# Two w_up products kept in PSUM for the convolution, and one difference of norm2 moved behind the broadcast

## The chip, the core and the metric

The kernel runs on one core of a Trainium2 chip. The core has five engines that are used here: TensorE (PE, matrix products into PSUM), VectorE (DVE), ScalarE (ACT), GpSimd (POOL, which works on SBUF) and SyncE (SP, which issues the DMAs). Each engine works through its own queue in order and waits on semaphores for the others. The metric is the device time of one execution in microseconds, as the median over runs; lower is better.

## The reference, cut to what matters

The program is one layer of an encoder with 1024 positions, 1024 channels and a hidden width of 2816: two kinds of attention and a gated merge, then a feed-forward part with a depthwise convolution. Only the second half is touched:

```python
x = x + gate1 * (merged @ w_out)
h2 = rmsnorm(x, g_ffn) * (1 + scale2) + shift2
u = depthwise_conv3(h2 @ w_up) + conv_b          # 1024 -> 5632 channels, 3 taps along the positions
u_val, u_gate = split(u, 2)
x = x + gate2 * ((gelu(u_gate) * u_val) @ w_down)
return rmsnorm(x, g_final)
```

## The kernel before

**Layout.** Channels lie on the 128 partitions, positions along the free dimension in two halves of 512. An fp32 product is made of three fp32r products of a high and a low part (weights high x data high, high x low, low x high). A split into the two parts is a copy on ACT (`L55`, `L768`, `L873`, `L942`) and a subtraction on POOL (`L56`) or DVE (`L769`, `L874`, `L943`).

**w_up, 22 jobs.** A job `t` makes 128 value channels and 128 gate channels over all 1024 positions. It uses a Strassen-like scheme with 7 products (`products`, `STEPS`) in place of 8: each product is 4 x 3 matmuls of 128x128 by 128x512 (`L822` to `L824`). The four results lie in four PSUM banks, called a, b, c, d in `"abcdacd"[j]`, of a pool of six (`pj`, bufs=6). [...] The running sums `t` and `v` are tiles of `wc` in SBUF (5 of them). After product 0, ACT copies bank a into `t` (`L828`). After product 1, DVE adds bank b to `t` (`L830`), after 2 it adds bank c and `t` into `v` (`L832`), after 3 it adds bank d and `v` (`L835`): the second half of the gate channels. After 4, bank a holds the first half of the value channels; after 5, bank c plus `t` is the second half of them (`L840`); after 6, bank d plus `t` is the first half of the gate channels (`L844`). Where the results of `L835` and `L844` go is what `in_psum` says: without it (all w_up jobs) into the `wc` tile of `v` and of `t`; with it (the w_down jobs) back into a PSUM bank, b and d.

**The convolution.** `done` hands each of the four results to `finish`. `conv_in` (`L1012`, ACT) multiplies a half by the middle tap and adds the bias, into a tile `ys` of `big`. `conv_taps` adds the two outer taps in six DVE instructions (`L1018`), each with a half or a part of it as one input and `ys` as the other and the output. The positions are stored so that a neighbour lies 256 columns away or in the other half; the six instructions read 512, 256 or 255 columns. Then gelu on ACT (`L1044`), the product with the value half on DVE (`L1045`), and a store to DRAM (`L1046`) for w_down. The first two jobs (`t < 2`) wait until both halves are there before `conv_in`. In the last job the convolution has a lower priority.

**The weights.** `a_operands` makes the four combinations of a job's weights: sums on POOL (`L786` to `L788`) and DVE (`L795`), and splits on ACT and POOL, in two pairs of buffers.

**norm2, ahead of w_up.** `out_tile` (w_out) leaves for each of 8 channel tiles the scaled second half of the positions in `m2[k]`; the first half is already normalised in `m1[k]`. POOL takes differences `m2[k] = m2[k+4] - m2[k]` for k = 0 to 2 (`L997`), DVE the fourth (`L1003`). PE sums the squares; `rstd_of` makes the reciprocal root (`L94` DVE, `L95` ACT, `L96` DVE); PE broadcasts it over the partitions (`L102`). Then a loop with a fixed order for ACT, DVE and POOL multiplies each `m2[k]` by the broadcast (`L1084`), builds the operands T2 (`L1086`, `L942`, `L943`), T1 (`L1088`, `L768`, `L769`) and T3, and on POOL the start of T4 (`L1095`). PE meanwhile does the two products of jobs 0 and 1 that need only the first half (B11 and B21), in an order that is written out by hand up to the end of this stage.

**What sets the order elsewhere.** Within `manual_schedule` the order is that of the code. Elsewhere a planner lays out each engine's queue when the program is built, by its own durations and by the priority of the code's order; a tile or bank is given out when the planner's simulation finds one free, and the waits for it are put into the program.

**The way into w_down.** Jobs of w_down come straight behind. Their data operands come from the stored activations: `b_operands` takes differences on POOL into `wc` tiles (`L892`) and back (`L893`), and `moved` makes each operand through a copy in a PSUM bank (`L872`), a high part (`L873`) and a low part (`L874`, DVE).

Of the kernel before, what the change touches and what calls it, by code (L numbers as in the profile page):

```python
# [12 lines left out]
OP = mybir.AluOpType  # L13
# [15 lines left out]
def hybrid_encoder(tc, xT, c, w_ada, small, w_in, w_v, p1_bias, p23_bias, na_bias, ln2_mult, ident, w_br, w_out,  # L29
                   w_up, w_down, out):  # L30
    nc = tc.nc
    act, dve, pool, pe, sp = nc.scalar, nc.vector, nc.gpsimd, nc.tensor, nc.sync
# [53 lines left out]
    def add_sums(pcol, sq, first, last, n=4):  # L86

        for t in range(n):
            pe.matmul(pcol[:, t:t + 1], sq[:, t * 128:(t + 1) * 128], ones, start=first and t == 0,
                      stop=last and t == n - 1, skip_group_check=True)  # L90
# [169 lines left out]
    with tc.manual_schedule(engines={e.engine for e in (sp, act, dve, pool, pe)}):  # L260
# [50 lines left out]
        for n in range(24):  # L311
            g, k = divmod(n, 8)
# [542 lines left out]
    def wide(dtype=FT):  # L855
        return keep.tile([128, 512], dtype, name="wc", bufs=5)

    def big(shape, dtype=FT):
        return keep.tile(shape, dtype, name="big", bufs=9)
# [85 lines left out]
    def out_tile(hf, m, sqa, scaled):  # L945

        cols = halves[hf]
        w = out_w.pop()
        if hf + m < KT:
            out_w.append(weights(w_out[(m + 1) % KT], (pool, pool)[hf or m == KT - 1]))  # L950
        p = ps.tile([128, 512], FT, name="pj", bufs=6)
        product(p, w, lambda k: [t[:, k, cols] for t in ms])
        xx = x2[hf][m]
        dve.scalar_tensor_tensor(xx, p, ada[:, 16 + m:17 + m], xx, OP.mult, OP.add)
        sp.dma_start(x_scr[m][:, cols], xx)
        sq = sqa if m == 0 else wide()
        if m == KT - 1:
            dve.tensor_tensor(sq, xx, xx, OP.mult)
        else:
            act.activation(sq, xx, AF.Square)  # L960
        act.activation(scaled, xx, AF.Copy, scale=am2[:, m:m + 1])
        if 0 < m < KT - 1:
            (dve if hf and m > 2 else pool).tensor_tensor(sqa, sqa, sq, OP.add)
        return sq

    def up_load(t):
        raw = []
        for i in range(2):
            r = big([128, KT, 128]) if t in (0,) or t > 1 and t % 2 else wpool.tile([128, KT, 128], FT, name="wraw")
            sp.dma_start(r, w_up[t + FF * i])  # L970
            raw.append(r.rearrange("p (a b) m -> p a b m", a=2))
        return raw
# [16 lines left out]
    m2 = []  # L989
# [10 lines left out]
    late_mm.enter_context(tc.manual_schedule(engines={pe.engine}))  # L1000
    m2.append(half_tile())
    sq = out_tile(1, KT - 1, sqa, m2[KT - 1])
    dve.tensor_tensor(m2[3], m2[7], m2[3], OP.subtract)  # L1003
    mpool.release()
    oppool2 = tc.alloc_tile_pool(name="ops2", bufs=1, side="right", reuse_waits="tile")
    for n in ("T2", "T1", "T3"):
# [3 lines left out]
    with tc.tile_pool(name="up", bufs=2, reuse_waits="tile") as work:  # L1010
        def conv_in(y, t, hf, src):
            act.activation(y[:, halves[hf]], src, AF.Identity, bias=conv[:, 3, t:t + 1], scale=conv[:, 1, t:t + 1])  # L1012

        def conv_taps(y, t, ph):
            w0, w2 = conv[:, 0, t:t + 1], conv[:, 2, t:t + 1]

            def tap(dst, src, wt):
                dve.scalar_tensor_tensor(y[:, dst], src, wt, y[:, dst], OP.mult, OP.add)  # L1018
            tap(slice(256, 768), ph[0], w0)
            tap(slice(768, 1024), ph[1][:, 0:256], w0)  # L1020
            tap(slice(1, 256), ph[1][:, 256:511], w0)
            tap(slice(0, 256), ph[0][:, 256:512], w2)
            tap(slice(256, 768), ph[1], w2)
            tap(slice(768, 1023), ph[0][:, 1:256], w2)

        def up_products(t, st, seq=range(7)):
            u, ys = [{}, {}], {i: big([128, S]) for i in range(2) if t == FF - 1}

            def done(i, hf, src):
                u[i][hf] = src  # L1030
                if len(u[i]) == 1 and t < 2:
                    return
                with tc.high_priority(offset=-300 if t == FF - 1 else 0):
                    finish(i, hf)

            def finish(i, hf):
                if i not in ys:
                    ys[i] = big([128, S])
                for n in range(2) if t < 2 else (hf,):
                    conv_in(ys[i], t + FF * i, n, u[i][n])  # L1040
                if len(u[i]) == 2:
                    conv_taps(ys[i], t + FF * i, u[i])
                if len(u[0]) + len(u[1]) == 4:
                    act.activation(ys[1], ys[1], AF.Gelu_apprx_tanh)  # L1044
                    dve.tensor_tensor(ys[0], ys[0], ys[1], OP.mult)  # L1045
                    sp.dma_start(a_scr[t], ys[0])  # L1046
            return products(st, 4, lambda n, k: late[n][k] if n in late else (ops[n][0][:, k], ops[n][1][:, k]), done,
                            seq)

        raw[1] = up_load(1)  # L1050
        prep = [a_operands(raw.pop(t), 4, lambda t: work, sts[t], dve) for t in range(2)]
        next(prep[0])
        next(prep[1])
        for _ in range(3):
            next(prep[0])
        next(prep[1])
        gens = [up_products(t, sts[t], (0, 4, 1, 2, 3, 5, 6)) for t in range(2)]

        def advance(g):
            for j in g:  # L1060
                if j >= 0:
                    return j

        pcol = ps.tile([128, 512], FT, name="pcol")
        add_sums(pcol, sqa, True, False)
        next(gens[0])
        add_sums(pcol, sq, False, True)
        advance(gens[0])
        bc = bcast(rstd_of(pcol, 4), ps, "pbc")
        advance(gens[1])  # L1070
        advance(gens[0])
        advance(gens[1])

        t2 = big([128, 2, 512])
        t2 = [t2[:, 0], t2[:, 1], wide(), wide()]

        def t_split(n, k, src, b):
            shifted(src, b, ops[n][0][:, k], ops[n][1][:, k])

        with tc.manual_schedule(engines={act.engine, dve.engine, pool.engine}):  # L1080

            for k in range(10):
                if k < 8:
                    dve.tensor_tensor(m2[k], m2[k], bc, OP.mult)  # L1084
                if 1 <= k < 5:
                    dve.tensor_tensor(t2[k - 1], m2[k - 1], m1[k - 1], OP.add)  # L1086
                elif k >= 5 and k < 9:
                    dve.tensor_tensor(m1[k - 5], m2[k - 1], t2[k - 5], OP.subtract)  # L1088
                if 2 <= k < 6:
                    t_split("T2", k - 2, t2[k - 2], shift2[:, 2 + k:3 + k])  # L1090
                elif k >= 6:
                    operand(m1[k - 6], ops["T1"][0][:, k - 6], ops["T1"][1][:, k - 6], dve)
            for k in range(4):
                t_split("T3", k, m2[k], dshift[:, k:k + 1])
                pool.tensor_tensor(m1[4 + k], m1[4 + k], t2[k], OP.subtract)  # L1095
            for k in range(4):
                late["B22"].append((half_tile(FR), half_tile(FR)))
                shifted(m2[4 + k], shift2[:, 4 + k:5 + k], *late["B22"][k])
            for k in range(4):
                late["T4"].append((half_tile(FR), half_tile(FR)))  # L1100
                operand(m1[4 + k], *late["T4"][k], pool)
        for g in gens:
            advance(g)
        late_mm.close()
        for t in range(FF):
            nxt = iter(())
            if t + 2 < FF:
                raw[t + 2] = up_load(t + 2)
            if 0 < t < FF - 1:
                nxt = a_operands(raw.pop(t + 1), 4, lambda t: work, sts[t + 1], last=t + 2 == FF)  # L1110
                next(nxt)
            elif t == 0:
                nxt = prep[1]
            for j in gens[t] if t < 2 else up_products(t, sts[t]):
                if j in (((2, 5), (2, 3, 5))[t] if t < 2 else (1, 2, 5)):
                    next(nxt, None)
                if t == FF - 1 and j == 0:
                    more = b_operands(0, movs[0])
                    next(more)
                if t == FF - 1 and j == 2:  # L1120
                    next(more)
                if t == FF - 1 and j == 3:
                    oppool2.release()
                    work2 = tc.alloc_tile_pool(name="down2", bufs=1, side="right", reuse_waits="tile")
                    reserve(work2, [(n + e, 2048, G) for n in ("B11", "T2", "T1") for e in "hl"]
                            + [("T3h", 2048, G), ("T3l", 2048, G)])
                    for _ in range(3):
                        next(more)
# [204 lines left out]
```

## Time and profile before

| | |
|---|---|
| time, median of three runs | 1574.42 us (1573.51 to 1581.34) |
| profiled execution: time, span | 1572.37 us, 1570.5 us |
| granted TensorE clock, mean | 0.982 |
| PE, DVE, ACT, POOL busy | 1505.5, 1035.6, 779.1, 740.6 us |
| w_up, from 1000 to 1320 us in the span | PE 320.00 of 320.00 us busy |
| conv taps `L1018` with a source in `wc` | 132 of them, mean 933 ns |
| conv taps `L1018` with a source in `pj` | 132 of them, mean 565 ns |

The span runs from the first to the last instruction of the profiled execution; its own time has a little around it. All positions in microseconds are counted from the start of the span. A row of the timeline has the start, the duration (of all instructions merged into the row), the engine, the line, the operation, the tile written and the tiles read, the shapes, the count, and in brackets the idle time before it with the engine and tile that ended the wait. PE's matmuls overlap: their durations of 0.39 us are longer than their spacing. `x` is the name of the tiles of the second half of norm2 too, `big` and `wc` are shared SBUF tiles, `pj` the PSUM banks of the products.

### The profile page before, as it was taken

How to read it: one execution, taken by the hardware profiler on the slowest of the kernel's cores; microseconds unless marked ns; L12 is line 12 of the kernel's file. 1: busy time of each engine (PE TensorE's matmuls, PEld its weight loads, DVE VectorE, ACT ScalarE, POOL GpSimd, SP SyncE). 2: the span in 40 equal slices, each digit the busy share in tenths (PEclk: the TensorE clock that was granted, in tenths of full speed). 3: DMA queues.
4: the chain of work that ended last, by engine and by line, in shares of the span. 5: the costliest groups of instructions: out<-in, count | busy, mean ns of one | idle time of the engine just before them, and what ended most of it. 6: DMA issues, size and time to landing. Idle time of an engine off the chain costs nothing.

```text
span 1570.5 us, 21187 instructions
## 1 busy us (share of the span) xinstructions
PE 1505.5 (96%) x7582; PEld 1267.3 (81%) x7582; DVE 1035.6 (66%) x1873; ACT 779.1 (50%) x1419; POOL 740.6 (47%) x475
## 2 busy tenths in 40 slices
PE   7998899999999999999999888999999999999998
PEld 6787788888888998887778777888888887778777
DVE  7694366576766655535534898776666667877765
ACT  3420466566765766643344454444444446575542
POOL 2310523233324444311145858676666665778621
PEclk8899999999999999999999999999999999999999
DMA  9577632323245565555544212322222224523313
GB/s 374 193 272 282 171 80 93 100 73 107 75 108 144 149 160 139 170 174 172 175 136 141 94 54 81 108 81 81 82 87 87 81 74 144 189 97 122 115 53 108
DMA packets 110001, 205.21 MB, mean 131 GB/s; under 512 B 40356, under 2 KB 55588, under 8 KB 109860
## 3 DMA queue, kind: packets, MB, share of 16 engines
q1 hardware_dynamic: 109624, 203.59, 40.3%
q8 instruction: 60, 0.98, 0.3%
q14 instruction: 45, 0.37, 0.1%
q10 hardware_dynamic: 272, 0.26, 0.1%
HBM read 158.73 MB, written 42.47 MB: 128 GB/s over the span
## 4 chain that ended last, share of the span: by engine, by line
PE 64%; DVE 12%; DMA 8%; POOL 6%; issue 4%; ACT 4%; SPq 1%; DVEq 0%; ACTq 0%; POOLq 0%
PE pj L822 8%; PE pj L823 8%; PE pj L824 8%; PE pj L79 8%; PE pj L77 8%; PE pj L78 8%; DMA g<-gs 2%; DMA wraw<-w_down 2%; PE pj L378 2%; DVE mt L151 2%; DVE big L1018 2%; PE O L672 2%; POOL wsl L56 2%; POOL wlo L56 1%; PE T L660 1%
## 5 line engine op out<-in xcount | busy, mean ns | idle before, releaser
L56 POOL TENSOR_TENSOR wlo<-wraw,whi 128x1024 fp32r<-128x1024 f32 (+1 forms) x77 | 178.9, 2323 | 249.6 <-ACT whi L55 224.4
L79 PE MATMUL pj<-h,wlo 128*128 128x512 f32 x448 | 178.6, 399 | 1.4 <-POOL wlo L56 1.4
L77 PE MATMUL pj<-h,whi 128*128 128x512 f32 x448 | 178.4, 398 | 0.1
L78 PE MATMUL pj<-h,whi 128*128 128x512 f32 x448 | 178.2, 398 | 0.0
L56 POOL TENSOR_TENSOR wsl<-big,wsh 128x1024 fp32r<-128x1024 f32 (+1 forms) x45 | 109.5, 2434 | 48.1 <-ACT wsh L55 48.0
L1018 DVE SCALAR_TENSOR_TENSOR big<-wc,sm,big 128x256 f32<-128x256 f32 (+1 forms) x132 | 116.8, 933 | 17.3 <-ACT big L1012 17.2
L55 ACT ACTIVATE whi<-wraw 128x1024 fp32r<-128x1024 f32 (+1 forms) x79 | 80.7, 1022 | 73.7 <-PE pj L78 30.0
L79 PEld LDWEIGHTS pj<-h,wlo 128*128 128x128 f32 x448 | 84.4, 188 | 16.3 <-POOL wlo L56 1.8
L78 PEld LDWEIGHTS pj<-h,whi 128*128 128x128 f32 x448 | 84.3, 188 | 14.4
L77 PEld LDWEIGHTS pj<-h,whi 128*128 128x128 f32 x448 | 84.4, 188 | 14.2 <-PE pj L79 0.5
L449 POOL TENSOR_TENSOR vv<-vv 96x256 fp32r<-96x256 f32 (+2 forms) x32 | 41.2, 1297 | 102.6 <-ACT vv L448 93.1
L498 ACT ACTIVATE P<-P,st 128x256 f32<-128x256 f32 x128 | 64.3, 503 | 49.6 <-DVE st L497 49.3
L385 POOL TENSOR_SCALAR qb<-qs 128x256 fp32r<-128x256 f32 x32 | 26.4, 851 | 124.0 <-PE S L544 57.9
L497 DVE CUSTOM_DVE_ANT_0 P<-S,bias 128x256 f32<-128x256 f32 x128 | 52.4, 421 | 42.3 <-PE S L544 23.2
L1018 DVE SCALAR_TENSOR_TENSOR big<-pj,sm,big 128x512 f32<-128x512 f32 x132 | 67.9, 565 | 16.1 <-ACT big L1012 16.1
L1012 ACT ACTIVATE big<-wc,sm 128x512 f32<-128x512 f32 x44 | 35.8, 816 | 75.7 <-DVE wc L835 45.3
L56 POOL TENSOR_TENSOR wsl<-wraw,wsh 128x768 fp32r<-128x768 f32 (+1 forms) x23 | 49.9, 2171 | 45.5 <-ACT wsh L55 45.5
L650 POOL TENSOR_SCALAR P<-P,stb 128x288 f32<-128x288 f32 (+1 forms) x32 | 39.9, 1248 | 66.0 <-DVE stb L647 58.8
L55 ACT ACTIVATE wsh<-big 128x1024 fp32r<-128x1024 f32 (+1 forms) x45 | 44.8, 1000 | 37.1 <-POOL big L787 23.6
L1044 ACT ACTIVATE big<-big 128x1024 f32<-128x1024 f32 x22 | 23.3, 1060 | 80.2 <-DVE big L1018 80.2
L503 DVE TENSOR_TENSOR tl<-T,th 128x512 fp32r<-128x512 f32 x64 | 43.7, 688 | 23.9 <-ACT th L502 23.5
L840 DVE TENSOR_TENSOR pj<-pj,wc 128x512 f32<-128x512 f32 x34 | 23.7, 696 | 47.0 <-PE pj L824 46.9
(366 smaller groups left out, 4862.3 us busy)
## 6 DMA issues: line engine op xcount, KB each, us to landing
wraw<-w_in SPq DMA_DIRECT2D x32, 512.0 KB, 4.2
t<-w_ada SPq DMA_DIRECT2D x24, 512.0 KB, 8.0
big<-w_up SPq DMA_DIRECT2D x22, 512.0 KB, 5.9
wraw<-w_up SPq DMA_DIRECT2D x22, 512.0 KB, 3.5
as<-big SPq DMA_DIRECT2D x22, 512.0 KB, 2.6
big<-as SPq DMA_DIRECT2D x22, 512.0 KB, 6.2
wraw<-w_down SPq DMA_DIRECT2D x24, 384.0 KB, 3.7
x<-w_ada SPq DMA_DIRECT2D x16, 512.0 KB, 9.9
```

Of the source, the lines that this page charges most:

```text
L55: act.activation(hi, raw, AF.Copy)
L56: lo_eng.tensor_tensor(lo, raw, f(hi), OP.subtract)
L77: pe.matmul(psum, whi[:, k0 + k], mhi, start=k == 0, stop=False)
L78: pe.matmul(psum, whi[:, k0 + k], mlo, start=False, stop=False)
L79: pe.matmul(psum, wlo[:, k0 + k], mhi, start=False, stop=k == n - 1)
L497: dve.tensor_tensor_reduce(pp, d, bias, -1.0, BIG, OP.add, OP.min, mi)
L498: act.activation(pp, pp, AF.Exp, bias=mi, scale=-1.0, accum_out=li)
L503: dve.tensor_tensor(tl, pt, f(th), OP.subtract)
L822: pe.matmul(psum, whi[:, k], bhi, start=j < 4 and k == 0, stop=False, skip_group_check=True)
L823: pe.matmul(psum, whi[:, k], blo, start=False, stop=False, skip_group_check=True)
L824: pe.matmul(psum, wlo[:, k], bhi, start=False, stop=k == n - 1, skip_group_check=True)
L1018: dve.scalar_tensor_tensor(y[:, dst], src, wt, y[:, dst], OP.mult, OP.add)
```

## The change

From the third job on (`t > 1`), `products` gets `in_psum`: `L835` writes its sum into bank b and `L844` into bank d, and `conv_in` and `conv_taps` read all four halves from PSUM. The first two jobs stay as they were. The other part moves the fourth difference of norm2, `m2[3] = m2[7] - m2[3]` on DVE, from ahead of the reciprocal root into the loop, just before `m2[3]` is multiplied by the broadcast.

```diff
@@ norm2
     sq = out_tile(1, KT - 1, sqa, m2[KT - 1])
-    dve.tensor_tensor(m2[3], m2[7], m2[3], OP.subtract)
     mpool.release()
@@ up_products
             return products(st, 4, lambda n, k: late[n][k] if n in late else (ops[n][0][:, k], ops[n][1][:, k]), done,
-                            seq)
+                            seq, t > 1)
@@ the loop behind the broadcast
             for k in range(10):
+                if k == 3:
+                    dve.tensor_tensor(m2[3], m2[7], m2[3], OP.subtract)
                 if k < 8:
                     dve.tensor_tensor(m2[k], m2[k], bc, OP.mult)
```

## The prediction, made before the changed kernel was run

> **What bounds the kernel now.** I read the page first, then the table of windows, then the stage around the change engine by engine. From the page:
>
> ```profile
> PE 1505.5 (96%) x7582; PEld 1267.3 (81%) x7582; DVE 1035.6 (66%) x1873; ACT 779.1 (50%) x1419; POOL 740.6 (47%) x475
> ```
>
> TensorE (PE) is busy 96% of the span, so an edit to VectorE (DVE) work can pay only where PE stands still. The windows say where, around norm2 and w_up:
>
> ```profile
> 880.00:935.00 55.00, 46.76 (x198) 37.43 (x198) 51.79 (x57) 24.56 (x38) 39.75 (x22) 0.94 0.14 49
> 935.00:1000.00 65.00, 60.54 (x258) 48.90 (x257) 56.81 (x65) 30.01 (x37) 47.04 (x24) 0.97 0.22 73
> 1000.00:1320.00 320.00, 320.00 (x1410) 264.30 (x1409) 223.36 (x325) 142.81 (x176) 215.30 (x121) 1.00 0.27 92
> 1320.00:1345.00 25.00, 20.46 (x78) 15.38 (x77) 22.10 (x36) 21.08 (x37) 13.85 (x12) 0.86 0.41 137
> ```
>
> The columns are length, then busy us (instructions) of PE, PEld, DVE, ACT, POOL, granted clock, DMA. From 1000 to 1320 PE is never idle: 1410 matmuls in 320 us, 0.227 us each. That is most of w_up, where most changed instructions lie; there the change can lose but not gain. At that rate the other rows lose 55 - 198 x 0.227 = 10.1 us, 65 - 258 x 0.227 = 6.4 us and 25 - 78 x 0.227 = 7.3 us: 23.8 us in all is the ceiling. PE's timeline gives the stalls behind them, with what ended each:
>
> ```profile
> 893.25 1.00 PE L102 MATMUL pbc<-idt,rs 128*128 128x128 f32 x4 [4.11 <-DVE rs L96]
> 908.90 0.50 PE L823 MATMUL pj<-T2lo,wsh 128*128 128x512 f32 x1 [2.41 <-DVE T2lo L943]
> 917.10 0.50 PE L823 MATMUL pj<-T1lo,wsh 128*128 128x512 f32 x1 [1.52 <-DVE T1lo L769]
> 956.69 0.50 PE L822 MATMUL pj<-B21hi,whi 128*128 128x512 f32 x1 [2.67 <-ACT wc L828]
> 980.38 0.50 PE L822 MATMUL pj<-x,big 128*128 128x512 f32 x1 [1.79 <-DVE wc L832]
> 1332.44 0.50 PE L823 MATMUL pj<-T2l,wsh 128*128 128x512 f32 x1 [1.67 <-DVE T2l L874]
> 1336.14 0.79 PE L823 MATMUL pj<-T1l,wsh 128*128 128x512 f32 x1 [2.72 <-DVE T1l L874]
> ```
>
> All but one end on DVE. So the question is what the edit does to DVE's queue at these seven places.
>
> **Part 1: the two products stay in PSUM (20 of 22 jobs).** Nothing is added: the additions of L835 and L844 write a PSUM bank instead of a wc tile, and ACT and DVE read the bank. The price of a conv tap (L1018) with its source in SBUF (wc) and in PSUM (pj), from the page and from the line's own view (min/median/max ns):
>
> ```profile
> L1018 DVE SCALAR_TENSOR_TENSOR big<-wc,sm,big 128x256 f32<-128x256 f32 (+1 forms) x132 | 116.8, 933 | 17.3 <-ACT big L1012 17.2
> L1018 DVE SCALAR_TENSOR_TENSOR big<-pj,sm,big 128x512 f32<-128x512 f32 x132 | 67.9, 565 | 16.1 <-ACT big L1012 16.1
> L1018 DVE SCALAR_TENSOR_TENSOR big<-wc,sm,big x132: 469/740/2897, 928.1 to 1336.7; 128x256 f32<-128x256 f32 x44, 128x255 f32<-128x255 f32 x44, 128x512 f32<-128x512 f32 x44
> L1018 DVE SCALAR_TENSOR_TENSOR big<-pj,sm,big x132: 467/476/754, 931.0 to 1334.0; 128x512 f32<-128x512 f32 x44, 128x256 f32<-128x256 f32 x44, 128x255 f32<-128x255 f32 x44
> ```
>
> Same shapes, same minimum; only the SBUF form ever takes 2.9 us. A DVE instruction with two SBUF inputs waits while POOL is inside one of its own; with one input in PSUM it doesn't. DVE loses 6 x (0.933 - 0.565) = 2.2 us of work a job, 44 us in all. Between 1000 and 1320 that is worth nothing, since PE covers it. It is worth something at two places.
>
> *Third job.* DVE between 965 and 981:
>
> ```profile
> 965.65 2.19 DVE L1018 SCALAR_TENSOR_TENSOR big<-pj,sm,big 128x512 f32<-128x512 f32 x4 [0.85 <-ACT big L1012]
> 969.13 1.45 DVE L1018 SCALAR_TENSOR_TENSOR big<-wc,sm,big 128x255 f32<-128x255 f32 x1
> 971.10 5.42 DVE L1018 SCALAR_TENSOR_TENSOR big<-wc,sm,big 128x512 f32<-128x512 f32 x3
> 976.45 2.88 DVE L795 TENSOR_TENSOR wraw<-wraw,big 128x512 f32<-128x512 f32 x1
> 979.65 0.68 DVE L832 TENSOR_TENSOR wc<-pj,wc 128x512 f32<-128x512 f32 x1
> ```
>
> Four taps of wc take 6.87 us; at 0.565 they take 2.26. L832, for which PE waits at 980.38, then starts some 4.6 us earlier, and PE stopped only 1.79 us before: the stall goes. What is late next is a bank (below) or nothing. I take -1.8; ends -1.8 and 0.
>
> *Second job.* The stall of 2.67 us at 956.69 stays: it hangs on ACT, which sits behind the gelu of job 1, which waits for these taps, and jobs 0 and 1 keep wc:
>
> ```profile
> 945.73 9.27 DVE L1018 SCALAR_TENSOR_TENSOR big<-wc,sm,big 128x256 f32<-128x256 f32 x6
> ```
>
> *Way into w_down.* POOL, then DVE:
>
> ```profile
> 1312.56 2.73 POOL L892 TENSOR_TENSOR wc<-big 128x512 f32<-128x512 f32 x2 [2.08 <-DVE big L1018]
> 1323.58 0.70 DVE L840 TENSOR_TENSOR pj<-pj,wc 128x512 f32<-128x512 f32 x1 [2.20 <-PE pj L824]
> 1327.03 2.12 DVE L1018 SCALAR_TENSOR_TENSOR big<-wc,sm,big 128x255 f32<-128x255 f32 x1
> 1332.91 1.52 DVE L1018 SCALAR_TENSOR_TENSOR big<-pj,sm,big 128x512 f32<-128x512 f32 x3
> ```
>
> DVE works without a pause from 1323.58 and the stalls at 1332.44 and 1336.14 (4.39 us) wait for its T2l and T1l. The tap at 1327.03 falls from 2.12 to 0.47: -1.65, on the path. POOL's L892 waits 2.08 us for taps to give wc tiles back; w_up will hold fewer wc tiles, so L892 and L893 and with them T2 come up to 2.08 earlier, and DVE has the idle 2.20 us to use it. I count half, -1.0. Against it: in its last job four banks stay with the taps, where L835 and L844 freed two, so the third product of w_down's first job waits for the taps that end at 1332.91 + 1.52 = 1334.43; but its low operand T1l only comes at 1336.14. Sum -2.65; ends -3.7 and +1.5 (that product then 1.5 us later than T1l's gain would allow).
>
> *The steady jobs: a bank in place of a copy.* A job takes 4 of 6 banks. Now two come free at L835 and L844 or sooner; after the change all four are held until their taps end. The next job finds two free banks, and its third product (T1) needs a third. In the program of before, the bank free longest is given out first: it will be one of the first pair, whose taps end at 1308.74 + 0.87 = 1309.61, 2.9 us before T1 starts:
>
> ```profile
> 1308.15 0.68 DVE L844 TENSOR_TENSOR wc<-pj,wc 128x512 f32<-128x512 f32 x1
> 1308.74 0.87 DVE L1018 SCALAR_TENSOR_TENSOR big<-pj,sm,big 128x256 f32<-128x256 f32 x2
> 1309.53 3.34 DVE L1018 SCALAR_TENSOR_TENSOR big<-wc,sm,big 128x255 f32<-128x255 f32 x5
> 1312.48 0.39 PE L822 MATMUL pj<-T1hi,wsh 128*128 128x512 f32 x1
> ```
>
> So I cost it at nothing, covered by 2.9 us a job. The second pair has until the job after next.
>
> **Part 2: the difference of norm2.** L1003 moves from ahead of the reciprocal into the loop, ahead of its fourth product with the broadcast. One DVE instruction, no DMA, no POOL or SP work moves. DVE, then ACT and POOL:
>
> ```profile
> 890.19 0.15 DVE L94 TENSOR_SCALAR rs<-pcol 128x4 f32<-128x4 f32 x1
> 890.27 2.75 DVE L1003 TENSOR_TENSOR x<-x,x 128x512 f32<-128x512 f32 x1
> 892.94 0.16 DVE L96 RECIPROCAL rs<-rs 128x4 f32<-128x4 f32 x1
> 894.29 1.29 DVE L1084 TENSOR_TENSOR x<-x,pbc 128x512 f32<-128x512 f32 x2 [1.18 <-PE pbc L102]
> 895.49 2.64 DVE L1086 TENSOR_TENSOR big<-x,big 128x512 f32<-128x512 f32 x1
> 909.37 0.68 DVE L1088 TENSOR_TENSOR big<-x,big 128x512 f32<-128x512 f32 x1
> 890.38 0.20 ACT L95 ACTIVATE rs<-rs 128x4 f32<-128x4 f32 x1 [0.64 <-DVE rs L94]
> 889.68 7.90 POOL L56 TENSOR_TENSOR wsl<-big,wsh 128x1024 fp32r<-128x1024 f32 x3
> ```
>
> The difference costs 0.68 us alone (as L1088 at 909.37); it took 2.75 because POOL is inside the first of three L56 of some 2.4 us. The reciprocal needs only the square root on ACT (L95), done at 890.58: it can go at 890.65, so the broadcast and the loop start 2.3 us earlier. But the loop is a DVE queue without a gap, and the difference is now in it: -2.3 + 0.68 = -1.6 at best. At worst more: POOL's three L56 still end near 897.6, so two L1086 instead of one fall under them, each waiting up to 2.4 us, and the difference itself may meet POOL's L1095. Replaying the queue by hand, DVE and POOL taking turns, I get the last T2lo, for which PE waits at 908.90, 1.5 us later than now. I take half, +0.7, since the turns after T2 fall otherwise too; ends -1.6 and +1.5.
>
> **Sum:** +0.7 - 1.8 - 2.65 = -3.75. The profiled execution took 1572.37 us with a span of 1570.5; that becomes about 1568.6. The median of the three runs stands 2.05 higher at 1574.42, so 1570.7 as a median.
>
> [...]
>
> **Rivals.**
> *All gains arrive.* Norm2 -1.6, third job -1.8, way into w_down -3.7, and without the stalls the granted clock there recovers (0.86 over 25 us is 3.5 us of full clock; about half of it fell on matmuls, as the 0.79 us at 1336.14 against 0.39 elsewhere shows: 1.8): -8.9, 1565.5. For it: the stalls all end on DVE. Against: POOL's turns. Chance 0.18.
> *Nothing arrives.* Norm2 +1.5; PE waits for a bank instead of L832 in the third job; way into w_down -0.5: 1575.4. For it: DVE is behind there, so banks come back late. Chance 0.22.
> *Banks bind: slower.* If the planner, which orders DVE and PE by its own durations, hands out the second pair first or puts other work ahead of the first pair's taps, T1 waits in each of 18 jobs. It decides from 2.9 us of lateness on; to pass +0.5% from -3.75 it takes 11.7 / 18 = 0.65 us a job. At 1 us a job: 1570.7 + 18 = 1588.7. [...] Chance 0.08.
>
> **Numbers.** The forecast has the remaining 0.52. 0.5% is 7.9 us, about what a measurement here can tell from no change: 1566.5 to 1582.3. Faster: 0.18 and a tail of the forecast, 0.20. Slower: 0.08. Same: 0.72. The range from 1563.5 to 1577.5 leaves out the banks (0.08), the far part of all gains (0.05) and the upper part of nothing (0.05).
>
> **What would show it.** L1018 on pj at 240 of 264, mean near 0.56, and 24 on wc. The 1.79 us stall before L822 at about 980 gone; that of 2.67 at about 956 still there. L96 right behind L95, the moved difference above 0.68 us, PE's wait for T2lo no shorter. 1000 to 1320 still without a PE gap; PE idle there behind a tap (L1018) would make the prediction wrong upwards, a clock of 1.00 and fewer than 4 us of stalls in w_down's first 20 us downwards.

## The result: 0.25% faster, as forecast, but by terms that came out otherwise

| | before | after |
|---|---|---|
| median of 20 runs each, side by side | 1575.18 us (1571.82 to 1581.34) | 1571.19 us (1566.19 to 1576.28) |
| ratio, 95% interval | | 0.9975 [0.9964, 0.9987] |
| profiled execution: time, span, mean clock | 1572.37, 1570.5, 0.982 | 1569.62, 1567.6, 0.983 |

The 3.99 us between the medians meet the 3.75 forecast. The two profiled executions, from which all rows below come, differ by 2.75 us. In the changed kernel the lines from L1004 to L1082 have numbers one smaller than before (taps L1017, gelu product L1044, store L1045), the moved difference is L1083, and what follows it has numbers one larger (multiplication L1085, T2 sums L1087).

The same four windows, same columns (length; busy us and instructions of PE, PEld, DVE, ACT, POOL; clock; DMA):

```profile
880.00:935.00 55.00, 47.52 (x199) 37.07 (x198) 51.74 (x58) 24.86 (x38) 40.34 (x22) 0.91 0.15 49
935.00:1000.00 65.00, 62.32 (x275) 51.04 (x274) 52.08 (x67) 31.95 (x40) 52.49 (x28) 1.00 0.29 98
1000.00:1320.00 320.00, 320.00 (x1409) 264.42 (x1408) 224.55 (x324) 141.72 (x177) 216.71 (x116) 1.00 0.25 87
1320.00:1345.00 25.00, 20.85 (x74) 15.04 (x73) 23.51 (x41) 21.53 (x39) 15.61 (x12) 0.86 0.42 136
```

By the prediction's rate of 0.227 us a matmul the lossy windows now lose 55 - 199 x 0.227 = 9.8 us (10.1 before), 65 - 275 x 0.227 = 2.6 (6.4) and 25 - 74 x 0.227 = 8.2 (7.3). The middle of w_up is still without a gap. The last window is not quite the same work in both, since w_down starts 3.6 us earlier now; the table further down counts by matmuls instead. PE's stalls in its timeline, with what ended each:

```profile
891.25 0.62 PE L102 MATMUL pbc<-idt,rs 128*128 128x128 f32 x4 [1.80 <-DVE rs L96]
903.99 0.50 PE L823 MATMUL pj<-T2lo,wsh 128*128 128x512 f32 x1 [2.72 <-DVE T2lo L943]
907.35 0.80 PE L823 MATMUL pj<-T2lo,wsh 128*128 128x512 f32 x1 [2.05 <-DVE T2lo L943]
909.70 0.80 PE L823 MATMUL pj<-T2lo,wsh 128*128 128x512 f32 x1 [0.70 <-DVE T2lo L943]
917.29 0.51 PE L823 MATMUL pj<-T1lo,wsh 128*128 128x512 f32 x1 [0.21 <-DVE T1lo L769]
956.91 0.50 PE L822 MATMUL pj<-B21hi,whi 128*128 128x512 f32 x1 [2.68 <-ACT wc L828]
1326.88 0.50 PE L822 MATMUL pj<-T2h,wsh 128*128 128x512 f32 x1 [2.12 <-ACT wsh L55]
1328.79 0.80 PE L824 MATMUL pj<-T2h,wsl 128*128 128x512 f32 x1 [0.27 <-POOL wsl L56]
1333.73 0.50 PE L823 MATMUL pj<-T1l,wsh 128*128 128x512 f32 x1 [1.77 <-DVE T1l L874]
```

Norm2's stalls have moved from the broadcast and T1 to T2, with about the same sum. The one at 956.91 stayed, the one near 980 is gone, and a new one of 2.12 us on weights (`wsh`) stands at the start of w_down.

PE's matmuls of w_up and w_down can be counted through in both traces (84 to a job) and the start of the n-th compared. The difference after minus before, read as a step at each stage, is the balance:

| stage, in matmuls of w_up and w_down | before, us | after, us | change | forecast |
|---|---|---|---|---|
| norm2: 0 to 84 | 33.15 | 33.05 | -0.10 | +0.7 |
| through the stalls at 957 and 980: 84 to 336 | 63.96 | 60.29 | -3.67 | -1.8 |
| steady, 18 jobs: 336 to 1848 | 343.77 | 343.67 | -0.10 | 0 |
| way into w_down: 1848 to 1932 | 26.87 | 27.53 | +0.66 | -2.65 |

The sum of the four is -3.2; with +0.3 at the first matmul that gives -2.91 at the 1932nd, and the spans end 2.9 us apart. After the change the matmul counted as 1848 is w_up's last, not w_down's first, since one matmul of w_down goes ahead of it; that is 0.2 us.

### The profile page after: what moved, and what is told of

The parts are those of the page before. It is cut to its first block, busy times and chain, and to the rows that moved or that the text cites. A ratio compares the mean times of both kernels' runs of the same rounds, so it can differ in the third digit from the quotient of the medians.

```text
span 1567.6 us, 21162 instructions
## 1 busy us (share of the span) xinstructions
PE 1505.0 (96%) x7582; PEld 1266.6 (81%) x7582; DVE 1030.4 (66%) x1873; ACT 777.7 (50%) x1419; POOL 748.4 (48%) x475
## 4 chain that ended last, share of the span: by engine, by line
PE 63%; DVE 12%; DMA 9%; POOL 6%; ACT 4%; issue 4%; SPq 1%; DVEq 0%; ACTq 0%; POOLq 0%
PE pj L822 8%; PE pj L823 8%; PE pj L824 8%; PE pj L79 8%; PE pj L77 8%; PE pj L78 8%; DMA wraw<-w_down 3%; DMA g<-gs 2%; DVE mt L151 2%; PE pj L378 2%; PE O L672 2%; POOL wlo L56 2%; POOL wsl L56 2%; DVE big L1017 1%; PE T L660 1%
## 5 line engine op out<-in xcount | busy, mean ns | idle before, releaser
L1017 DVE SCALAR_TENSOR_TENSOR big<-pj,sm,big 128x512 f32<-128x512 f32 (+2 forms) x252 | 128.4, 565 | 33.1 <-ACT big L1011 33.1
L1011 ACT ACTIVATE big<-pj,sm 128x512 f32<-128x512 f32 x84 | 63.1, 776 | 123.6 <-DVE pj L840 55.6
L1044 DVE TENSOR_TENSOR big<-big 128x1024 f32<-128x1024 f32 x22 | 49.7, 2259 | 23.6 <-ACT big L1043 23.6
L56 POOL TENSOR_TENSOR wsl<-wraw,wsh 128x768 fp32r<-128x768 f32 (+1 forms) x23 | 54.5, 2371 | 12.8 <-ACT wsh L55 12.8
L795 DVE TENSOR_TENSOR wraw<-wraw,big 128x384 f32<-128x384 f32 (+1 forms) x23 | 35.3, 1537 | 34.7 <-POOL big L787 26.5
L79 PE MATMUL pj<-mhi,wlo 128*128 128x512 f32 x128 | 50.7, 396 | 1.8 <-POOL wlo L56 1.8
```

The costliest lines, as they stand in the source:

```text
L56: lo_eng.tensor_tensor(lo, raw, f(hi), OP.subtract)
L79: pe.matmul(psum, wlo[:, k0 + k], mhi, start=False, stop=k == n - 1)
```

## The experiments

All ratios are against the kernel before, run on the same chip. A difference in a stage between two profiles says something from some 0.5 us on: E1, whose norm2 is that of before, took 32.70 us there and before 33.15. Where a stretch of slow matmuls comes or goes with the execution (below), it takes 1.6 us with it.

### Each part alone

**E1, the products in PSUM alone.**

```diff
@@ up_products, in the kernel before
-                            seq)
+                            seq, t > 1)
```

> Part 1 alone: in_psum from the third job on, the difference of norm2 stays ahead of the reciprocal. Theory (the gain is the third job's stall): the 1.79 us stall of PE on L832 near 980 is gone, PE reaches the 336th matmul of w_up 2 to 3.6 us earlier than before and stays there to the end of w_up, w_down starts with a new wait on wsh of some 2 us, total 2 to 4 us under before. Rival (the moved difference carries part of it): total at most 2 us under before. Rival (banks bind): PE gaps between 1000 and 1320, total above before.

Measured: 1572.76 us against 1575.71, ratio 0.9976 [0.996, 0.9992]. The stall near 980 is gone and that on `wsh` is there:

```profile
1325.50 0.50 PE L822 MATMUL pj<-T2h,wsh 128*128 128x512 f32 x1 [2.11 <-ACT wsh L55]
```

So the first part alone shows the gain in the total and the new wait.

**E2, the moved difference alone** (the change without `t > 1`).

> Part 2 alone: the difference behind the broadcast, all w_up jobs keep wc. Theory (one DVE queue, nothing saved): the reciprocal comes 2.3 us earlier, the last T2lo as late as before within 0.6 us, the 1.79 us stall near 980 still there, w_down's start without the wait on wsh; total within 1 us of before. Rival (the head's gain goes through): the last T2lo and everything behind it 1.6 us earlier, total 1.6 us under before.

Measured: 1576.63 us against 1575.71, ratio 0.9999 [0.9982, 1.0016]. Norm2 took 33.07 us (before 33.15): PE's wait for the broadcast fell from 4.11 to 1.80 us and came back in waits for T2. The second part is worth nothing here. Its profile is useful for another reason, the third job, where `wc` is as before:

```profile
958.66 0.50 PE L822 MATMUL pj<-B21hi,whi 128*128 128x512 f32 x1 [2.69 <-ACT wc L828]
982.37 0.50 PE L822 MATMUL pj<-x,big 128*128 128x512 f32 x1 [3.42 <-DVE wc L832]
```

The wait for L832 is 3.42 us instead of 1.79, and yet the stretch from matmul 84 to 336 took 64.04 us, as long as before. The answer is in the matmuls right behind the stall at 957, here in the kernel before and then in the changed one:

```profile
958.59 0.63 PE L823 MATMUL pj<-B21lo,whi 128*128 128x512 f32 x1
959.02 0.63 PE L824 MATMUL pj<-B21hi,wlo 128*128 128x512 f32 x1
```

```profile
958.63 0.39 PE L823 MATMUL pj<-B21lo,whi 128*128 128x512 f32 x1
958.86 0.39 PE L824 MATMUL pj<-B21hi,wlo 128*128 128x512 f32 x1
```

In the first pair matmuls start 0.43 us apart, in the second 0.23. In the profile of before eight matmuls have the slow spacing, 8 x 0.2 = 1.6 us, and the granted clock from 958.6 to 962.4 is 0.60; in E2's and in that of after there are none and it is 1.00. In before this slow stretch came ahead of the wait for L832 and was taken out of it: 1.79 + 1.6 is E2's 3.42. DVE's lateness in the third job was therefore 3.4 us of PE's time, of which the profile of before labelled only half as a wait.

**E4, the change without the difference of norm2.**

```diff
-                if k == 3:
-                    dve.tensor_tensor(m2[3], m2[7], m2[3], OP.subtract)
```

> The changed kernel with the fourth difference of norm2 left out altogether (m2[3] is used as it is), to see what it costs in its new place. Theory (it waits for POOL in DVE's queue): the last T2lo comes 1.8 us earlier than in the changed kernel, being the 1.77 us that the instruction took there, and PE's waits for T2lo shrink by about as much; total 1 to 2 us under the changed kernel, 4.5 to 6 under before. Rival (it is covered in the new place): last T2lo and total as in the changed kernel.

Measured: 1569.7 us against 1575.71, ratio 0.9964 [0.9947, 0.9981]. Norm2 took 32.33 us, 0.72 less than in after, so the 1.77 us that the difference takes there, from DVE's timeline of the changed kernel,

```profile
893.11 2.61 DVE L1087 TENSOR_TENSOR big<-x,big 128x512 f32<-128x512 f32 x1
896.25 2.29 DVE L1087 TENSOR_TENSOR big<-x,big 128x512 f32<-128x512 f32 x1
898.46 1.79 DVE L943 SCALAR_TENSOR_TENSOR T2lo<-big,ada,T2hi 128x512 fp32r<-128x512 f32 x1
900.18 1.77 DVE L1083 TENSOR_TENSOR x<-x,x 128x512 f32<-128x512 f32 x1
908.91 0.74 DVE L943 SCALAR_TENSOR_TENSOR T2lo<-wc,ada,T2hi 128x512 fp32r<-128x512 f32 x1
```

costs PE at most some 0.7, less than the 1.8 us expected of PE's waits, and hardly above what two profiles differ by. The rows also bear out the prediction's reason for a loss: two T2 sums L1087 now take over 2 us instead of one (2.61 and 2.29 us against 0.68 alone).

### Where the way into w_down lost

The new wait is for `wsh`, the weights of w_down's first job. Behind it is the sum L786, which waits for a `big` tile until a store has read it. First the store of w_up's last job but one and that L786 in the kernel before, then in the changed one:

```profile
1316.39 0.32 SPq L1046 DMA_DIRECT2D as<-big  x1
1319.98 1.29 POOL L786 TENSOR_TENSOR big<-wraw 128x384 f32<-128x384 f32 x1
```

```profile
1317.49 0.32 SPq L1045 DMA_DIRECT2D as<-big  x1
1320.55 1.02 POOL L786 TENSOR_TENSOR big<-wraw 128x384 f32<-128x384 f32 x1 [4.17 <-DMA as<-big]
```

Matmul 1848 starts at 1326.10 before and 1322.53 after, so the store has slid from 9.7 us ahead of it to 5.0. The cause is in PE's queue: the last two products of that job (`x,big`, 24 matmuls) stand behind other work now. Before, the next job (B11) follows them; after, B11 and two matmuls of T2 come ahead of them:

```profile
1301.57 0.39 PE L822 MATMUL pj<-x,big 128*128 128x512 f32 x1
...
1307.01 0.39 PE L822 MATMUL pj<-B11hi,whi 128*128 128x512 f32 x1
```

```profile
1300.50 0.39 PE L824 MATMUL pj<-B11hi,wlo 128*128 128x512 f32 x1
1300.73 0.39 PE L822 MATMUL pj<-T2hi,wsh 128*128 128x512 f32 x1
1300.95 0.39 PE L823 MATMUL pj<-T2lo,wsh 128*128 128x512 f32 x1
1301.18 0.39 PE L822 MATMUL pj<-x,big 128*128 128x512 f32 x1
```

That is 14 matmuls or 3.2 us. The other 1.5 us lie behind the job's last matmul, which starts 9.6 us ahead of the store before and 11.1 after. Both programs have such an order at matmul 312 of w_up; the kernel before is back in the order of the code from about matmul 430 on, the changed one keeps it to the end. A job's results come later, and in the steady jobs PE doesn't wait for them. The next runs put the order of before back.

**E9, the change with PE's queue in the order of the code from `t == 4` on.**

```diff
+        ordered = contextlib.ExitStack()
         for t in range(FF):
+            if t == 4:
+                ordered.enter_context(tc.manual_schedule(engines={pe.engine}))
...
     for p in oppools[::-1]:
         p.release()
+    ordered.close()
```

> The changed kernel with PE's order written out by hand from the fifth job of w_up to its end (job by job, as the kernel before had it there), in place of the planner's, which puts the first product of the next job and two matmuls of the second ahead of the last two products of each job. Theory (the gain on the way into w_down went into that order: the last products come 14 matmuls or 3.2 us later, so the taps, the gelu, the store and the big tile for w_down's first weights do): the 2.12 us wait for wsh at w_down's start is gone, w_down's 24th matmul is reached 2 to 4 us earlier against w_up's end, total 5 to 8 us under before. Rival (the banks held by the last job make the wait): the wait on wsh stays, total as the changed kernel, 3 to 4 us under before. Rival (the planner's order was needed to cover DVE): new PE gaps between 980 and 1320, total above the changed kernel.

Measured: 1571.61 us against 1575.71, ratio 0.9967 [0.9953, 0.9982]. The wait for `wsh` is gone and the way into w_down took 25.08 us (before 26.87, after 27.53). The window from matmul 1848 to 1932, in E9 and then in the changed kernel:

```profile
1329.73:1354.81 25.08, 21.95 (x86) 16.47 (x84) 24.88 (x40) 20.98 (x37) 14.62 (x11) 0.93 0.43 144
1322.53:1350.06 27.53, 23.38 (x85) 17.12 (x84) 26.55 (x45) 22.34 (x39) 15.27 (x12) 0.88 0.41 131
```

The same matmuls in 2.45 us less, at a clock of 0.93 instead of 0.88. But the total is 4.1 us under before, where 5 to 8 were expected: the manual order begins with a wait for a bank that the taps still hold, and eight slow matmuls behind it, and the steady stretch (336 to 1848) took 347.77 us in place of 343.67:

```profile
989.78 0.50 PE L822 MATMUL pj<-T1hi,wsh 128*128 128x512 f32 x1 [2.23 <-DVE big L1017]
```

**E10, the same from `t == 8` on.**

> The changed kernel with PE's order by hand from the ninth job of w_up to its end, so that DVE is no longer behind where the order by hand begins. Theory (the order by hand from the fifth job paid 2.23 us of a bank wait and 1.6 us of slow clock at its start, and won 1.8 us at w_down's start where the changed kernel loses 0.7): no PE gap between 980 and 1320, w_down's 84th matmul some 1.8 us earlier against w_up's end than in the kernel before, total 2 to 3 us under the changed kernel, 5.5 to 7 under before. Rival (the bank wait comes wherever the order by hand begins): a gap of about 2 us near the ninth job, total as with the order from the fifth job.

Measured: 1572.57 us against 1576.08, ratio 0.9972 [0.9952, 0.9992]: 3.5 us under before, where 5.5 to 7 were expected. There is no gap from 980 to 1320, and the way into w_down took 25.20 us. Its waits:

```profile
1333.92 0.50 PE L822 MATMUL pj<-T1h,wsh 128*128 128x512 f32 x1 [0.53 <-DVE big L1017]
1334.80 0.47 PE L822 MATMUL pj<-T3h,wsh 128*128 128x512 f32 x1 [0.38 <-DVE big L1017]
1337.61 0.79 PE L823 MATMUL pj<-T1l,wsh 128*128 128x512 f32 x1 [2.11 <-DVE T1l L874]
```

The first two are banks that w_up's last taps hold, which the prediction named as the counter-term. They suggested leaving the last job with `wc`:

**E11, E10 with the last job through SBUF.**

```diff
-                            seq, t > 1)
+                            seq, 1 < t < FF - 1)
```

> As the order by hand from the ninth job, and the last job of w_up keeps wc as before, so that two of its banks come free at the additions. Theory (the four banks that the last job holds cost PE the waits of 0.52 and 0.38 us on conv taps at w_down's start): these two waits are gone, total 0.5 to 1.5 us under the order from the ninth job with all in PSUM. Rival (T1l and T2l on DVE set that stretch, and taps from wc make them later): the waits for T1l grow by what the bank waits shrink, total the same or up to 1.5 us above.

Measured: 1569.89 us against 1576.08, ratio 0.9957 [0.9941, 0.9972]. The waits for banks are gone, but those for T2l and T1l are back at 1.68 and 2.73 us, as before the change (1.67 and 2.72); the way into w_down took 27.17 us, 0.3 more than before. By the trace the idea fell: there, taps from PSUM save DVE more than the banks cost PE. The median, 2.7 us under that of E10, points the other way; the intervals overlap, and on the second set of runs (below) E10 is the lower one.

**E12, E10 with job 1 in PSUM too** (`t > 0`), against the stall at 957.

> As the order by hand from the ninth job, with in_psum from the second job on instead of the third. Theory (the six taps of the second job from wc, 9.3 us behind POOL, make the 2.7 us stall near 957): its taps take 3 to 4 us, that stall is gone, total 2 to 4 us under the order from the ninth job alone. Rival (with two jobs interleaved by hand six banks are too few once the second holds four): PE waits on conv taps between 935 and 960 by as much or more, total the same or above.

Measured: 1570.44 us against 1576.08, ratio 0.9961 [0.9944, 0.9977]. That stall is gone, and two others stand in its place:

```profile
936.11 0.50 PE L822 MATMUL pj<-T3hi,wsh 128*128 128x512 f32 x1 [0.90 <-DVE big L1017]
943.23 0.49 PE L822 MATMUL pj<-x,wsh 128*128 128x512 f32 x1 [1.34 <-DVE pj L835]
```

Matmuls 84 to 336 took 60.10 us, as in E10 (60.24), so the 2.1 us by which the median lies under E10's are not won there. The run shows something else at w_down's start: its waits are those of E10 (0.53, 0.38 and 2.11 us), yet the way into w_down took 26.61 us in place of 25.20. Behind the last wait 13 matmuls had the slow spacing of 0.43 us instead of 7, and the granted clock over the stage was 0.87 instead of 0.93.

**E7, the change with five banks instead of six** (`bufs=5` for `pj`), for the rival in which banks bind.

> The changed kernel with five banks for the products instead of six, in every stage that uses this pool; only the stretch of w_up from the seventh job on is read. Theory (six banks leave a margin): the third product still finds its bank in time, PE has no gap from 1010 to 1310. Rival (six banks are just enough): PE waits on conv taps (L1017) in every job, by 1 us a job or more, 15 us in all.

Measured, one run: 1596.73 us. From 1000 to 1320 PE waits for the taps once a job; a row of the waits (line, what it waits for, total us, times, longest):

```profile
PE pj L822 <- DVE big L1017: 14.1, 16, 1.0
```

From matmul 336 to 1848 it takes 20.4 us longer than before, 1.13 us for each of 18 jobs. The rival's mechanism is real and its price of 1 us a job was about right; with six banks it doesn't show in the steady jobs under the planner's order, and shows once where the order by hand begins (E9, 2.23 us).

**After, E10 and E11 once more, on one chip.**

> The changed kernel itself once more, beside the two with PE's order by hand, so that all three share one chip and the runs of the kernel before. Expected as on its first runs, 0.25% under before; PE loses between the 84th and the 336th matmul of w_up either 0 or 1.6 us more than 57.3 us of matmuls and the 2.7 us stall near 957, by whether the clock falls behind that stall.

> PE's order by hand from the ninth job, all in PSUM from the third on. Theory (the way into w_down is 2.4 us shorter with it): 2 us, some 0.15%, under the changed kernel on the same chip. Rival (later stretches of w_down, which the planner lays out anew, take it back): as the changed kernel.

> PE's order by hand from the ninth job and wc in the last job. By its trace it lost the 2 us at w_down's start again, so theory: 0 to 1 us under the changed kernel. Rival (its first median, the lowest of all, was no chance): 2 us or more under it.

Measured against 1575.85 us: after 1570.17, 0.9973 [0.9959, 0.9988]; E10 1568.12, 0.9957 [0.9941, 0.9973]; E11 1569.53, 0.9969 [0.9952, 0.9986]. The way into w_down took 27.36, 25.08 and 27.15 us. So with the order of PE's queue held and all four results in PSUM, the way into w_down is 2.2 to 2.5 us shorter than in the changed kernel's profiles in E9, E10 and E10 again, but only 0.8 to 0.9 shorter in E12, at its lower clock. PE's waits there sum to 3.0 us in all four, in place of 4.0 to 4.2 in the changed kernel's profiles and 4.4 before. In the totals the medians of this set differ by 2.05 us in favour of E10 over after, while the first pair of E10 against after's own runs did not show it, and the intervals overlap: as a whole E10 is faster than before, and not shown to be faster than after.

## Why the prediction was right, step by step

**Right in the sum, and in what bounds.** 1570.7 forecast, 1571.19 measured. PE's stalls behind DVE were the place to look, and the steady jobs gave back nothing. That the sum was met so closely is luck: three of the four terms were mis-sized, the third job brought 1.9 us more and norm2 0.8 more than forecast, and the way into w_down 3.3 less.

**Steady jobs, 0: right, for its reason.** E7 shows the bank wait with one bank less. One step within it was wrong for this program: DVE did not lose 44 us of work. DVE's groups from 1000 to 1320, before and then after (count, busy us, mean ns, idle before):

```profile
L1018 DVE SCALAR_TENSOR_TENSOR big<-wc,sm,big 128x512 f32<-128x512 f32 (+1 forms) x103 | 85.5, 880 | 15.1 <-ACT big L1012 15.0
L1018 DVE SCALAR_TENSOR_TENSOR big<-pj,sm,big 128x512 f32<-128x512 f32 (+2 forms) x102 | 52.7, 565 | 14.4 <-ACT big L1012 14.4
L1045 DVE TENSOR_TENSOR big<-big 128x1024 f32<-128x1024 f32 x17 | 21.9, 1289 | 10.0 <-ACT big L1044 10.0
L795 DVE TENSOR_TENSOR wraw<-wraw,big 128x512 f32<-128x512 f32 x8 | 6.7, 834 | 0.0
L795 DVE TENSOR_TENSOR big<-big 128x512 f32<-128x512 f32 x8 | 6.5, 818 | 1.5 <-POOL big L787 1.5
```

```profile
L1017 DVE SCALAR_TENSOR_TENSOR big<-pj,sm,big 128x512 f32<-128x512 f32 (+1 forms) x203 | 103.5, 565 | 28.0 <-ACT big L1011 28.0
L1044 DVE TENSOR_TENSOR big<-big 128x1024 f32<-128x1024 f32 x17 | 41.8, 2458 | 21.2 <-ACT big L1043 21.2
L795 DVE TENSOR_TENSOR wraw<-wraw,big 128x512 f32<-128x512 f32 x8 | 14.1, 1763 | 16.2 <-POOL big L787 11.9 <-DMA big<-w_up 4.3
L795 DVE TENSOR_TENSOR big<-big 128x512 f32<-128x512 f32 x8 | 14.1, 1760 | 15.2 <-POOL big L787 15.2
```

The taps fell by 34.7 us (138.2 to 103.5), the 565 ns a tap came as forecast; but the instructions that still read SBUF twice, the gelu product and the weight sums, took 34.9 us more (35.1 to 70.0). The wait for POOL was not removed, it was handed on. That it cost nothing is PE's cover.

The timelines of DVE and POOL show the wait that the prediction names. In the kernel before 44 of the 132 taps from `wc` start while POOL is inside an instruction: each of them ends 0.28 to 0.55 us after that instruction does, and they take up to 2.90 us. Of the 132 taps from `pj` 121 start so, 92 of these end before POOL's instruction, and none takes more than 0.75 us. Of the 22 gelu products 3 start inside a POOL instruction in the kernel before and 18 in the changed one; these take 1.40 to 2.83 us and end 1.08 to 1.09 us after that instruction, the others take 1.22 to 1.23 us.

The handing on hangs on the order of the queues. The same rows in E9, where PE's order is that of the code:

```profile
L1017 DVE SCALAR_TENSOR_TENSOR big<-pj,sm,big 128x256 f32<-128x256 f32 (+2 forms) x204 | 103.9, 564 | 29.5 <-ACT big L1011 28.0 <-DMA big<-as 0.8
L1044 DVE TENSOR_TENSOR big<-big 128x1024 f32<-128x1024 f32 x17 | 21.5, 1263 | 8.5 <-ACT big L1043 8.5
```

Here the product takes no more than before (1263 ns against 1289), nor do the weight sums (752 and 699 ns), and DVE as a whole is busy for 189.57 us in the window, in place of 223.36 before and 224.55 after. E9 differs from the changed kernel only in PE's order, to which the planner fits the other queues. So with the order of before the forecast saving does arrive; with the planner's order for the changed kernel the other instructions that read SBUF twice took it up. In E10, by hand from the ninth job only, the product takes 1503 ns.

**Third job, -1.8 forecast, -3.67 measured: right mechanism, mis-sized.** L832 starts at 973.35 in place of 979.65 and the four taps have shrunk as reckoned:

```profile
969.20 2.58 DVE L1017 SCALAR_TENSOR_TENSOR big<-pj,sm,big 128x512 f32<-128x512 f32 x5
971.69 1.74 DVE L795 TENSOR_TENSOR wraw<-wraw,big 128x512 f32<-128x512 f32 x1
973.35 0.68 DVE L832 TENSOR_TENSOR wc<-pj,wc 128x512 f32<-128x512 f32 x1
```

The step that failed is "PE stopped only 1.79 us before: the stall goes", with -1.8 as the end of the range. The slow stretch at 958 had hidden the other 1.6 (E2). Whether that second part is won depends on the clock of the execution: with the products in PSUM the stretch took 60.2 to 60.3 us in five profiles (after, E10, E11, after and E10 again) and 61.75 to 61.92 where the slow matmuls were there (E4, E9, E11 again; 63.3 in E1, which has a second slow stretch at matmuls 84 to 91). So the term is worth 2.1 us in some executions and 3.7 in others.

**Way into w_down, -2.65 forecast, +0.66 measured: the step that was wrong.** Its parts are there when PE keeps the order of the code: in E9 and E10 the stage gained 1.8 and 1.7 us on before, with the bank waits of the counter-term at 0.9. Of that, 1.4 us are shorter waits (4.39 to 3.0); the rest goes with the clock of the execution, and in E12, with the same waits, a gain of 0.3 was left. (DVE does not work quite without a pause there, as the prediction has it: it stands still for 0.36 us ahead of 1326.30, which changes none of this.) What the prediction missed is that the planner's order of PE's queue changes with this edit: 14 matmuls stand ahead of each job's last two products, a store comes 4.7 us later against PE, and with it L786, `wsh` and a wait of 2.1 us. It was argued that L892 gets its tile earlier; the tile that mattered was a `big` one, and it came later. Why the planner chose this order was not settled; the other holding of banks and `wc` tiles is the likely reason, not shown.

**Norm2, +0.7 forecast, -0.10 measured.** The two ends were -1.6 and +1.5 and the sum lies between. E2 and E4 agree that it is near nothing. The replay by hand foresaw too great a delay: the last T2lo ends at 909.65 in place of 908.84, and as the stage starts 0.3 us later, that is 0.5 us later and not 1.5. PE got this back at T1, where its wait fell from 1.52 to 0.21. Also, the count of taps on PSUM came out at 252 instead of 240, since jobs 0 and 1 had six each already; that touched no term.

**The rivals.** Banks bind in the steady jobs with five of them (E7), not with six. "All gains arrive" failed at the way into w_down, and "nothing arrives" at the third job. Leaving two more results of a job in PSUM cost the taps nothing: E1, which does only that, is 0.24% faster, and its taps from PSUM take 563 ns on average against 565 before.

## What to carry to other kernels

Where PE stands still behind DVE, read the matmul spacing ahead of the stall as well as the stall: a slow stretch just before it can hide a part of the lateness (here 1.6 of 3.4 us), and removing the cause can then be worth more than the row says (3.67 us for a row of 1.79). When a buffer's lifetime changes under a planner, compare the order of every queue near the stage ends, not only the instructions that were edited. A wait for POOL that one group of DVE instructions no longer has can turn up in another group when the order of the queues moves (here 34.7 us off the taps, 34.9 us on the gelu products and weight sums): sum the busy times of all groups that read SBUF twice, before and after. And compare a stage in several profiles before its time is put down to an edit, for with the same waits of PE the way into w_down took 25.20 us in one and 26.61 in another, by the slow matmuls behind the waits.

## What was not expected of the hardware

**Behind the same stall the granted clock fell in some executions only.** The stall at 957 was 2.62 to 2.71 us in every profile with six banks except E12's, where it is gone. Behind it about eight matmuls were 0.43 us apart (1.6 us in all) in before, E1, E4, E9 and E11 again, and 0.23 apart in after, E2, E10, E11, after again and E10 again: 5 of 11 have the slow stretch. E9's wait of 2.23 us at 989.78 had one behind it too, at a granted clock of 0.57 from 990 to 994. From 958.6 to 962.4 the granted clock was 0.60 in before and 1.00 in after, behind stalls of 2.67 and 2.68 us. What decides between the two was not shown.
